# Turning q, k and the softmax's weights of one encoder layer by VectorE and DRAM transfers in place of TensorE

## The chip, the core and the metric

The kernel runs on one core of a Trainium2 chip. The core has a matrix engine (TensorE, "PE" in the profile; its weight loads are listed apart as "PEld"), VectorE ("DVE"), ScalarE ("ACT"), GpSimd ("POOL") and SyncE ("SP"), which here only issues transfers. On-chip memory is SBUF (128 partitions); TensorE writes to PSUM. The metric is device time in microseconds (us), lower is better. A measurement is the median of several runs.

## The reference, cut to what matters

A bidirectional encoder of two layers, batch 1, 256 tokens, width 2048, all in float32. Each layer is a parallel mixer and a convolutional feed-forward net, both modulated by a conditioning vector:

```python
mod = c_act @ ada_w[l] + ada_b[l]                        # 6 x 2048 values
h = rmsnorm(x, norm_mix[l]) * (1.0 + sc_a) + sh_a
qa, ka, va, qb, kb, vb, ga, gb = split_cols(h @ w_in[l])
qa = rotary_partial(rmsnorm(qa.reshape(B, S, HA, HEAD_DIM), qn_a[l]), pos)
ka = rotary_partial(rmsnorm(ka.reshape(B, S, GA, HEAD_DIM), kn_a[l]), pos)
ya = window_attention(qa, ka, va, sink_a[l]) @ w_proj_a[l]      # 8 heads, 2 kv groups
qb = rmsnorm(qb.reshape(B, S, HB, HEAD_DIM), qn_b[l])
kb = rmsnorm(kb.reshape(B, S, HB, HEAD_DIM), kn_b[l])
yb = neighbourhood_attention(qb, kb, vb, rel_bias_b[l]) @ w_proj_b[l]   # 8 heads
merged = jax.nn.sigmoid(ga) * ya + jax.nn.sigmoid(gb) * yb
x = x + gt_a * (merged @ w_out[l])
h = rmsnorm(x, norm_ffn[l]) * (1.0 + sc_m) + sh_m
u = depthwise_conv(h @ w_up[l], conv_w[l], conv_b[l])
g, v = jnp.split(u, 2, axis=-1)
x = x + gt_m * ((jax.nn.silu(g) * v) @ w_down[l])
```

Both attentions are softmax attention over the 256 tokens with a mask or a bias: with heads of 128, `scores = q k^T`, `p = softmax(scores)`, `o = p v`. TensorE contracts over partitions, so the scores need q and k with the head's 128 values on the partitions, and the output needs p with the keys on the partitions. What the projections give has tokens on the partitions, and so do the scores. Hence q, k and p must be transposed ("turned").

## The kernel before, in words

**Weights.** All weight matrices of a layer lie in DRAM as one stream of 128x128 blocks, in the order of their use. A *unit* is 16 blocks, 1 MB. `unit_steps` loads a unit with one transfer from SyncE's queue (L286, the tile "w", a pool "raw" of four buffers) and splits it into two *halves* of eight blocks. A half is float32 values parted in a rounded part and a rest: ScalarE casts the rounded part (L297), VectorE subtracts it from the value (L298); both land in "hl", a pool of four halves. Each product on TensorE is three matmuls (part x part, rest x part, part x rest).

**Loops.** `features` keeps the result with features on the partitions: per block three matmuls (L314, L315, L316) of 128x256. `tokens` keeps tokens on the partitions: per four blocks six matmuls (L377 to L379) of 128x512. Results lie in PSUM ("ps", "ps_t"), and an evacuation function takes them out.

**The second layer's mixer**, unit by unit: units 0 to 7 hold half of the gate of branch A; units 8 to 43 hold q, k and v in nine token groups of four units each (`QKV_GROUPS`); units 44 to 51 hold the rest of A's gate; units 52 to 59 the projection of A (L403 gates it); units 60 to 75 the gate of B; from 76 on come the projection of B, the output projection and the feed-forward net. Beside it, "aw" loads (L225, the same "raw" buffers and the same queue) with one VectorE reduction each (L226) compute the modulation; a plan (`ADA_PLAN_1`) sets how many are done at which unit.

**A group of q and k.** A token group is four heads of 128 (the k group of A two heads, with v in its other columns, copied out at L896). `qk_rows` squares the rows on ScalarE (L547, one per head and half of the tokens), takes the root (L440 on VectorE, L441 on GpSimd), multiplies it in ("qn", L556), applies the rotation to A's (L571 to L573), and then turns them: `turn` transposes every 128x128 block on TensorE with the identity (L580) into PSUM, and ScalarE copies the result with the norm's gain as scale into "packA" or "packB" (L581). Each part comes some ticks after the one before: `bg.defer` puts a function off to the next tick, and there is a tick at every end of a unit.

**A head.** `attend` is a generator. Scores on TensorE (L607, "sc"); row maximum with mask or bias on VectorE (L610); the negative (L615); exp on ScalarE (L618, sum in the same instruction; A's heads also L621 and L622 for the sink); reciprocal (L624) and scaling (L626). After a yield, four transposes on TensorE (L631) into "tp", which are split as above into "pT" (`split`, L389 on ScalarE and L390 on VectorE; pT has one buffer). After a yield the output on TensorE ("po", L639) and its split into "oA" or "oB" (L641, L642). q, k and v of a head are split likewise (`in_halves`; "qh", "kh", "vh" have one buffer each). "p" has two buffers. A head of B loads its bias into p (L825). `attention` advances every living head by one yield a step; `bg.tick` calls it with a rate per unit, `ATT[1]` = 0.4 steps up to the projection of A and `ATT_B[1]` = 0.21 from there on. `attended(HA)` drives the A heads to their end before the projection of A, and `bg.finish(job)` the B heads before unit 76.

**What sets the order.** Every engine takes its instructions from a queue in order, and so does SyncE with the transfers. The order in a queue is not that of the program text: a planner arranges the instructions when the kernel is built, by dependences, by priorities (program order, where nothing else is said) and by its own estimate of each instruction's time. On the chip the queues are then served in that fixed order, with semaphores between them.

Of the kernel before, what the change touches and what calls it, by code (L numbers as in the profile page):

```python
# [9 lines left out]
F32 = mybir.dt.float32  # L10
F32R = mybir.dt.float32r
AF = mybir.ActivationFunctionType
# [3 lines left out]
P = 128  # L16
L = 2
D = 2048
S = 256
KC = D // P  # L20
HEAD = 128
HA, GA, HB = 8, 2, 8
# [5 lines left out]
NEG = -1e30  # L28
SCALE = HEAD ** -0.5
GRID_W, NA_KH, NA_KW = 64, 8, 16  # L30


QKV_GROUPS = [1024, 0, 512, 2560, 3584, 1536, 3072, 4096, 2048]
# [45 lines left out]
H_RATE = [2.7, 1.7]  # L79

ATT = [1.288, 0.4]
ATT_B = [0.21, 0.21]

SCORES_3 = (1,)

ADA_ORDER = [[p * KC + k for k in range(KC) for p in ps] for ps in ((0, 1), (2,), (3, 4), (5,))]
ADA_ORDER = [i for part in ADA_ORDER for i in part]
# [47 lines left out]
def encoder(ctx: ExitStack, tc: tile.TileContext, a: dict, out: bass.AP):  # L135
# [16 lines left out]
    sm = pool("sm", 3)  # L152
    mm = pool("mm", 4, space=bass.MemoryType.PSUM)
    ax = pool("ax", 3, space=bass.MemoryType.PSUM)

    ident = const.tile([P, P], F32, name="ident")
    make_identity(nc, ident[:])
# [378 lines left out]
            nc.vector.tensor_tensor(out=z[:], in0=ps[:, :S], in1=self.rbs[:], op=ALU.mult)  # L536
            return z, sh

    def qk_rows(pss, heads, rot, gain, dst, then):

        cols = 0
        n = heads * HEAD
        ss = sm.tile([P, 8], F32, name="qss", tag="qss")
        for t, ps in enumerate(pss):
            for i in range(heads):
                sq = at.tile([P, HEAD], F32, name="qsq", tag="qsq", bufs=1)
                nc.scalar.activation(  # L547
                    out=sq[:], in_=ps[:, cols + i * HEAD : cols + (i + 1) * HEAD], func=AF.Square,
                    accum_out=ss[:, t * heads + i : t * heads + i + 1],
                )  # L550
        rs = sm.tile([P, 8], F32, name="qrs", tag="qrs")
        rsqrt(rs[:, : 2 * heads], ss[:, : 2 * heads], HEAD, 2 * heads)
        def norm():
            qn = at.tile([P, 2, 4, HEAD], F32, name="qn", tag="qn", bufs=1)
            for t, ps in enumerate(pss):
                nc.vector.tensor_tensor(  # L556
                    out=qn[:, t, :heads],
                    in0=ps[:, cols : cols + n].rearrange("p (h d) -> p h d", d=HEAD),
                    in1=rs[:, t * heads : (t + 1) * heads].unsqueeze(2).broadcast_to([P, heads, HEAD]),
                    op=ALU.mult,  # L560
                )
# [12 lines left out]
            bg.defer(lambda: turn(qn))  # L574

        def turn(qn):
            for t in range(2):
                ps = ax.tile([P, 4, P], F32, name="qtp", tag="ax")
                for h in range(heads):
                    nc.tensor.transpose(ps[:, h], qn[:, t, h], ident[:])  # L580
                nc.scalar.activation(  # L581
                    out=dst[:, :, t * P : (t + 1) * P], in_=ps[:, :heads], func=AF.Identity, scale=gain
                )
            then()

        bg.defer(lambda: bg.defer(lambda: bg.defer(norm)))
# [12 lines left out]

        return ((0, 0), (0, 1), (1, 0))[: 2 * len(x) - 1]  # L600

    def attend(q, k, v, p, mask, scale, sink, o):

        sc = ax.tile([P, 2, S], F32, name="sc", tag="ax")
        for t in range(2):
            for i, j in by(q):
                nc.tensor.matmul(sc[:, t], q[i][:, t * P : (t + 1) * P], k[j], start=i + j == 0, stop=(i, j) == by(q)[-1])  # L607
        m = sm.tile([P, 2], F32, name="m", tag="m")
        for t in range(2):
            nc.vector.tensor_tensor_reduce(  # L610
                out=p[:, t], in0=sc[:, t], in1=mask[:, t], scale=scale, scalar=-3.0e38 if sink is None else sink,
                op0=ALU.add, op1=ALU.max, accum_out=m[:, t : t + 1],
            )
        nm = sm.tile([P, 2], F32, name="nm", tag="nm")
        nc.vector.tensor_scalar(out=nm[:], in0=m[:], scalar1=-1.0, scalar2=None, op0=ALU.mult)  # L615
        den = sm.tile([P, 2], F32, name="den", tag="den")
        for t in range(2):
            nc.scalar.activation(out=p[:, t], in_=p[:, t], func=AF.Exp, bias=nm[:, t : t + 1], accum_out=den[:, t : t + 1])  # L618
# [5 lines left out]
        nc.vector.reciprocal(out=ri[:], in_=den[:])  # L624
        for t in range(2):
            nc.scalar.activation(out=p[:, t], in_=p[:, t], func=AF.Copy, scale=ri[:, t : t + 1])  # L626
        yield
        tp = ax.tile([P, 2, S], F32, name="tp", tag="ax")
        for k in range(2):
            for t in range(2):  # L630
                nc.tensor.transpose(tp[:, k, t * P : (t + 1) * P], p[:, t, k * P : (k + 1) * P], ident[:])  # L631
        pT = at.tile([P, 2, 2, S], F32R, name="pT", tag="pT", bufs=1)
        split(pT, tp[:])
        v = v()
        yield
        po = ax.tile([P, 512], F32, name="po", tag="ax")
        for i, j in by(v):
            for b in range(2):
                nc.tensor.matmul(po[:, :S], v[i][:, b], pT[:, j, b], start=i + j + b == 0, stop=i + b == 2)  # L639
        o = o()  # L640
        nc.scalar.copy(o[:, 0], po[:, :S])  # L641
        nc.vector.tensor_tensor(out=o[:, 1], in0=po[:, :S], in1=o[:, 0].bitcast(F32), op=ALU.subtract)  # L642
# [115 lines left out]
    for l in range(L):  # L758
# [41 lines left out]
        def head_a(i):  # L800
            g = i // (HA // GA)
            if i >= 6:
                oA.append(paired(F32R, f"oA{l}_{i}"))
            elif i % 2 == 0:
                o = place(("y0", "y1", "y2")[i // 2], 4, F32R, f"oA{l}_{i}")
                oA.extend((o[:, :2], o[:, 2:]))
            q = in_halves(qTa[:, i], f"qA{l}_{i}", "qh", l in SCORES_3)
            if i % (HA // GA) == 0:
                kvs[0] = in_halves(kTa[:, g], f"kA{l}_{g}", "kh", l in SCORES_3)
            k = kvs[0]  # L810
            yield
            p = at.tile([P, 2, S], F32, name="p", tag="p")

            def v():
                if i % (HA // GA) == 0:
                    kvs[1] = in_halves(packs[0][:, 1:4:2, g * HEAD : (g + 1) * HEAD], f"vA{l}_{g}", "vh", True)
                return kvs[1]

            yield from attend(q, k, v, p, tables[0], SCALE, sink[:, i : i + 1], lambda: oA[i])

        def head_b(hb):
            b, i = packs[1 + hb // 4], hb % 4
            v = b[:, 4:8].rearrange("p (t a) s -> p t (a s)", t=2)
# [5 lines left out]
            yield from attend(  # L829
                q, k, lambda: in_halves(v[:, :, i * HEAD : (i + 1) * HEAD], f"vB{l}_{hb}", "vh", True), p, p, 1.0, None,  # L830
                lambda: oB_of(hb),
            )

        def oB_of(hb):
# [36 lines left out]
        for pi, (groups, gates) in enumerate(parts):  # L871
            last = pi == len(parts) - 1
            for g, part in enumerate(groups):
# [21 lines left out]
                    for t in range(2):  # L895
                        nc.scalar.copy(rows[:, t, vcol:], pss[t][:, vcol:])  # L896
                if g == 0:
                    qk_rows(pss, GA, rots[1], gains[:, 1:2], kTa, turned)
                elif g < 3:
                    qk_rows(pss, 4, rots[0], gains[:, 0:1], dst, turned)  # L900
                elif vcol is None:
                    qk_rows(pss, 4, None, gains[:, 3:4] if g in (3, 6) else gains[:, 2:3], dst, turned)
                else:
                    turned()
                if g == 2:
# [243 lines left out]
```

## Time and profile before

| | before |
|---|---|
| median of three runs | 2663.79 us (2663.64 to 2665.55) |
| the profiled execution, its span | 2663.2 us |
| TensorE busy | 2650.9 us |
| VectorE busy | 2102.2 us |
| ScalarE busy | 1412.8 us |
| GpSimd busy | 36.2 us |
| traffic with DRAM | 697 MB read and written through the transfer queue, 71.4% of 16 DMA engines |
| granted TensorE clock | full in each of 40 slices |

The profiled execution's own time is its span, 2663.2 us; that is 0.6 us under the median of the runs. The second layer's mixer up to the last B head lies at about 1394 to 1806 us of the span. In the rows below, "out<-in" gives the tiles by their names in the program, "x24" is the number of instructions, and after a bar come the busy time of the group, the mean of one in ns and the idle time just before them, with what ended most of it. In a row of a chain or of a timeline, the first two numbers are start and length in us; a bracket gives the idle time ahead and what ended it.

### The profile page before, as it was taken

Reading aid. Unit: us, or ns where it says so; the run is one execution under the profiler, and the core shown is the slowest. Engines: PE = TensorE matmul, PEld = TensorE weight load, DVE = VectorE, ACT = ScalarE, POOL = GpSimd, SP = SyncE. Lnnn points to the kernel's source line nnn. Section 1 sums busy time; section 2 is a strip of 40 time slices with the busy share of each in tenths; the row PEclk is TensorE's granted clock in tenths of the full one; section 3 lists DMA queues with packets and bytes.
Section 4 is the critical chain, followed back from the end, with each engine's and each line's share of the span. In section 5 each row is a group of like instructions: output and inputs, shape, how many; then the busy total and the mean of one; then the engine's idle time right before and its main releaser. Section 6 shows DMA issues by size and latency. Waiting matters only on the chain.

```text
span 2663.2 us, 50845 instructions
## 1 busy us (share of the span) xinstructions
PE 2650.9 (100%) x21256; PEld 2565.7 (96%) x21256; DVE 2102.2 (79%) x2959; ACT 1412.8 (53%) x2284; POOL 36.2 (1%) x25
## 2 busy tenths in 40 slices
PE   9999999999999999999999999999999999999999
PEld 7888899999999999999998889999999999999999
DVE  8898998997987888788976667768888866655664
ACT  5445865456644555355555566554565445544553
POOL 0001100000000000000000000000000000000000
PEclk9999999999999999999999999999999999999999
DMA  9987789885787878788766666666747765555554
GB/s 372 351 327 292 262 300 352 317 320 199 291 294 287 302 288 295 289 294 289 290 217 254 228 229 231 245 252 253 285 173 288 297 256 190 190 194 194 197 191 143
DMA packets 102039, 700.41 MB, mean 263 GB/s; under 512 B 12721, under 2 KB 15025, under 8 KB 17969
## 3 DMA queue, kind: packets, MB, share of 16 engines
q1 hardware_dynamic: 101810, 697.17, 71.4%
q8 instruction: 166, 2.72, 0.4%
q14 instruction: 63, 0.52, 0.1%
HBM read 695.03 MB, written 2.10 MB: 262 GB/s over the span
## 4 chain that ended last, share of the span: by engine, by line
PE 89%; DVE 6%; ACT 1%; issue 1%; DMA 1%; POOL 0%; SPq 0%; DVEq 0%; ACTq 0%
PE ps L314 25%; PE ps L316 25%; PE ps L315 25%; PE ps_t L377 4%; PE ps_t L379 4%; PE ps_t L378 4%; DVE hl L298 2%; DVE aw L226 2%; DMA aw<-in_aw 1%; PE sc L607 1%; PE po L639 1%; ACT hl L297 1%; PE tp L631 1%; POOL qrs L441 0%; PE qtp L580 0%
## 5 line engine op out<-in xcount | busy, mean ns | idle before, releaser
L298 DVE TENSOR_TENSOR hl<-w,hl 128x1024 fp32r<-128x1024 f32 x928 | 1128.3, 1222 | 360.0 <-ACT hl L297 357.6
L297 ACT CAST hl<-w 128x1024 fp32r<-128x1024 f32 x928 | 970.7, 1049 | 748.5 <-PE ps L316 518.1
L314 PE MATMUL ps<-h,hl 128*128 128x256 f32 x3328 | 922.8, 277 | 1.3 <-DVE ya L915 0.6
L315 PE MATMUL ps<-h,hl 128*128 128x256 f32 x3328 | 919.8, 276 | 0.0
L316 PE MATMUL ps<-h,hl 128*128 128x256 f32 x3328 | 919.8, 277 | 0.0
L314 PEld LDWEIGHTS ps<-h,hl 128*128 128x128 f32 x3328 | 624.8, 188 | 2.4 <-DVE ya L915 0.8
L315 PEld LDWEIGHTS ps<-h,hl 128*128 128x128 f32 x3328 | 625.3, 188 | 0.4 <-DVE h L470 0.2
L316 PEld LDWEIGHTS ps<-h,hl 128*128 128x128 f32 x3328 | 624.4, 188 | 0.0
L226 DVE CUSTOM_DVE_ANT_0 aw<-aw,cact,ab 128x2048 f32<-128x2048 f32 x189 | 443.5, 2347 | 48.8 <-DMA aw<-in_aw 47.8
L377 PE MATMUL ps_t<-hl,h 128*128 128x512 f32 x576 | 223.1, 392 | 2.6 <-ACT h L469 2.1
L378 PE MATMUL ps_t<-hl,h 128*128 128x512 f32 x576 | 224.9, 391 | 0.3
L379 PE MATMUL ps_t<-hl,h 128*128 128x512 f32 x576 | 224.3, 390 | 0.0
L994 DVE SCALAR_TENSOR_TENSOR u<-ps,cw,u 128x255 f32<-128x255 f32 x304 | 146.1, 481 | 66.5 <-ACT u L992 62.2
L992 ACT ACTIVATE u<-ps,cw 128x256 f32<-128x256 f32 x152 | 85.9, 565 | 187.9 <-PE ps L316 187.5
L316 PE MATMUL ps<-merged,hl 128*128 128x256 f32 x512 | 141.8, 277 | 0.4 <-DVE hl L298 0.4
L315 PE MATMUL ps<-merged,hl 128*128 128x256 f32 x512 | 141.6, 277 | 0.0
L314 PE MATMUL ps<-merged,hl 128*128 128x256 f32 x512 | 141.6, 277 | 0.0
L315 PE MATMUL ps<-act_o,hl 128*128 128x256 f32 x512 | 141.4, 276 | 0.0
L316 PE MATMUL ps<-act_o,hl 128*128 128x256 f32 x512 | 141.3, 276 | 0.0
L314 PE MATMUL ps<-act_o,hl 128*128 128x256 f32 x512 | 141.2, 276 | 0.0
L377 PEld LDWEIGHTS ps_t<-hl,h 128*128 128x128 f32 x576 | 107.9, 188 | 26.1 <-ACT h L469 3.1
L378 PEld LDWEIGHTS ps_t<-hl,h 128*128 128x128 f32 x576 | 108.1, 188 | 23.7 <-DVE hl L298 1.9
(231 smaller groups left out, 4612.5 us busy)
## 6 DMA issues: line engine op xcount, KB each, us to landing
w<-in_ws SPq DMA_DIRECT2D x463, 1024.0 KB, 4.9
aw<-in_aw SPq DMA_DIRECT2D x189, 1024.0 KB, 6.1
p<-in_bias SPq DMA_DIRECT2D x16, 256.0 KB, 4.2
x<-in_xT SPq DMA_DIRECT2D x4, 512.0 KB, 5.3
aw_o<-in_aw SPq DMA_DIRECT2D x2, 1024.0 KB, 12.3
out<-x SPq DMA_DIRECT2D x16, 128.0 KB, 2.1
w<-in_ws SPq DMA_DIRECT2D x2, 512.0 KB, 11.7
aw_b<-in_aw SPq DMA_DIRECT2D x1, 1024.0 KB, 18.1
```

The costliest lines, as they stand in the source:

```text
L226: nc.vector.tensor_tensor_reduce(out=raw[:], in0=raw[:], in1=cact[:], scale=1.0, scalar=ab[:, i : i + 1], op0=ALU.mult, op1=ALU.add, accum ...
L297: nc.scalar.copy(hl[:, 0], r)
L298: nc.vector.tensor_tensor(out=hl[:, 1], in0=r, in1=hl[:, 0].bitcast(F32), op=ALU.subtract)
L314: nc.tensor.matmul(out, hi, act[0], start=first, stop=False)
L315: nc.tensor.matmul(ps[:, :S], hi, act[1], start=False, stop=False)
L316: nc.tensor.matmul(out, lo, act[0], start=False, stop=last)
L377: nc.tensor.matmul(ps[:], xh, hi, start=kc == kcs[0], stop=False)
L378: nc.tensor.matmul(ps[:], xh, lo, start=False, stop=False)
L379: nc.tensor.matmul(ps[:], xl, hi, start=False, stop=kc == kcs[-1])
L607: nc.tensor.matmul(sc[:, t], q[i][:, t * P : (t + 1) * P], k[j], start=i + j == 0, stop=(i, j) == by(q)[-1])
L992: nc.scalar.activation(out=u, in_=ps, func=AF.Identity, scale=w[:, 1:2], bias=w[:, 3:4])
L994: nc.vector.scalar_tensor_tensor(out=u[:, to], in0=ps[:, of], scalar=w[:, j : j + 1], in1=u[:, to], op0=ALU.mult, op1=ALU.add)
```

## The change

In the second layer (`MOVED = (1,)`) neither q and k nor p go through TensorE for the turning; the first layer keeps its transposes.

VectorE's `transpose` turns each 32x32 block of a tile within itself. What is left is to move whole blocks to their places. `scatter` writes one 32-partition band of such a tile to a scratch tile in DRAM, 32 values (128 bytes) at a time, so that the tile in DRAM is the full transpose; then one transfer loads it back. A q or k group takes two VectorE turns of 128x512 (128x256 for the k group), eight scatters and one load into its place in "pack", on SyncE's queue, and then one ScalarE scaling with the gain instead of two copies from PSUM. A head takes one VectorE turn of 128x512, eight scatters and one load into the place of pT's rest; the split into pT then reads SBUF in place of PSUM. The load back and the scaling are each put off by a further tick; in a head there is one more yield, ahead of the load. The rate of the heads past the projection of A, `ATT_B[1]`, goes from 0.21 to 0.32 steps a unit. The scratch tiles come from a pool of two buffers per tag.

```diff
-ATT_B = [0.21, 0.21]
+ATT_B = [0.21, 0.32]
+BLOCK = 32
+MOVED = (1,)
...
+    dram = pool("dram", 2, space=bass.MemoryType.DRAM)
...
+    def scatter(y, src, t, a):
+        rows = y[:].rearrange("(b i) n (t a j) -> t a i n b j", i=BLOCK, t=2, a=P // BLOCK)
+        nc.sync.dma_start(rows[t, a], src[a * BLOCK : (a + 1) * BLOCK])
...
         def turn(qn):
+            if moved:
+                flat = qn[:, :, :heads].rearrange("p t h d -> p t (h d)")
+                for t in range(2):
+                    nc.vector.transpose(out=flat[:, t], in_=flat[:, t])
+                y = dram.tile([P, heads, S], F32, name="qY", tag="qY")
+                for t in range(2):
+                    for a in range(4):
+                        scatter(y, qn[:, t, :heads].rearrange("p h (b j) -> p h b j", j=BLOCK), t, a)
+                def back():
+                    nc.sync.dma_start(dst, y[:])
+                    def scaled():
+                        nc.scalar.activation(out=dst, in_=dst, func=AF.Identity, scale=gain)
+                        then()
+                    bg.defer(scaled)
+                bg.defer(back)
+                return
...
+    def once(fn):
+        due = [fn]
+        def run():
+            if due:
+                due.pop()()
+        return run
...
-        tp = ax.tile([P, 2, S], F32, name="tp", tag="ax")
-        for k in range(2):
+        if moved:
+            flat = p[:].rearrange("p t k -> p (t k)")
+            nc.vector.transpose(out=flat, in_=flat)
+            y = dram.tile([P, 2, S], F32, name="pY", tag="pY")
             for t in range(2):
-                nc.tensor.transpose(tp[:, k, t * P : (t + 1) * P], p[:, t, k * P : (k + 1) * P], ident[:])
-        pT = at.tile([P, 2, 2, S], F32R, name="pT", tag="pT", bufs=1)
-        split(pT, tp[:])
+                for a in range(4):
+                    scatter(y, p[:, t].rearrange("p (k b j) -> p k b j", k=2, j=BLOCK), t, a)
+            yield
+            pT = at.tile([P, 2, 2, S], F32R, name="pT", tag="pT", bufs=1)
+            whole = pT[:, 1].bitcast(F32)
+            nc.sync.dma_start(whole, y[:])
+            halve = once(lambda: split(pT, whole))
+            bg.defer(halve)
+        else:
...
         v = v()
         yield
+        if moved:
+            halve()
         po = ax.tile([P, 512], F32, name="po", tag="ax")
...
-            yield from attend(q, k, v, p, tables[0], SCALE, sink[:, i : i + 1], lambda: oA[i])
+            yield from attend(q, k, v, p, tables[0], SCALE, sink[:, i : i + 1], lambda: oA[i], l in MOVED)
...
-                    qk_rows(pss, 4, rots[0], gains[:, 0:1], dst, turned)
+                    qk_rows(pss, 4, rots[0], gains[:, 0:1], dst, turned, l in MOVED)
```

The branch under `else:` in `attend` is the old one. The call sites of B's heads and of the other groups get the same last argument.

More of the change, by code (lines that the diff above doesn't have):

```diff
@@ L537, in level, with qk_rows @@
             return z, sh
-    def qk_rows(pss, heads, rot, gain, dst, then):
+    def scatter(y, src, t, a):
+        rows = y[:].rearrange("(b i) n (t a j) -> t a i n b j", i=BLOCK, t=2, a=P // BLOCK)
+        nc.sync.dma_start(rows[t, a], src[a * BLOCK : (a + 1) * BLOCK])
+    def qk_rows(pss, heads, rot, gain, dst, then, moved=False):
         cols = 0
@@ L600, in by, with attend @@
         return ((0, 0), (0, 1), (1, 0))[: 2 * len(x) - 1]
-    def attend(q, k, v, p, mask, scale, sink, o):
+    def once(fn):
[4 more added lines that the diff above has]
+        return run
+    def attend(q, k, v, p, mask, scale, sink, o, moved=False):
         sc = ax.tile([P, 2, S], F32, name="sc", tag="ax")
@@ L627, in attend @@
         yield
-        tp = ax.tile([P, 2, S], F32, name="tp", tag="ax")
-        for k in range(2):
+        if moved:
+            flat = p[:].rearrange("p t k -> p (t k)")
+            nc.vector.transpose(out=flat, in_=flat)
+            y = dram.tile([P, 2, S], F32, name="pY", tag="pY")
             for t in range(2):
-                nc.tensor.transpose(tp[:, k, t * P : (t + 1) * P], p[:, t, k * P : (k + 1) * P], ident[:])
-        pT = at.tile([P, 2, 2, S], F32R, name="pT", tag="pT", bufs=1)
-        split(pT, tp[:])
+                for a in range(4):
[7 more added lines that the diff above has]
+        else:
+            tp = ax.tile([P, 2, S], F32, name="tp", tag="ax")
+            for k in range(2):
+                for t in range(2):
+                    nc.tensor.transpose(tp[:, k, t * P : (t + 1) * P], p[:, t, k * P : (k + 1) * P], ident[:])
+            pT = at.tile([P, 2, 2, S], F32R, name="pT", tag="pT", bufs=1)
+            split(pT, tp[:])
         v = v()
         yield
+        if moved:
+            halve()
         po = ax.tile([P, 512], F32, name="po", tag="ax")
@@ L830, in head_b @@
                 q, k, lambda: in_halves(v[:, :, i * HEAD : (i + 1) * HEAD], f"vB{l}_{hb}", "vh", True), p, p, 1.0, None,
-                lambda: oB_of(hb),
+                lambda: oB_of(hb), l in MOVED,
             )
@@ L897, in encoder @@
                 if g == 0:
-                    qk_rows(pss, GA, rots[1], gains[:, 1:2], kTa, turned)
+                    qk_rows(pss, GA, rots[1], gains[:, 1:2], kTa, turned, l in MOVED)
                 elif g < 3:
-                    qk_rows(pss, 4, rots[0], gains[:, 0:1], dst, turned)
+                    qk_rows(pss, 4, rots[0], gains[:, 0:1], dst, turned, l in MOVED)
                 elif vcol is None:
-                    qk_rows(pss, 4, None, gains[:, 3:4] if g in (3, 6) else gains[:, 2:3], dst, turned)
+                    qk_rows(pss, 4, None, gains[:, 3:4] if g in (3, 6) else gains[:, 2:3], dst, turned, l in MOVED)
                 else:
```

## The prediction

> **What bounds the kernel now.** The page comes first: busy time, then the slices.
>
> ```profile
> span 2663.2 us, 50845 instructions
> PE 2650.9 (100%) x21256; PEld 2565.7 (96%) x21256; DVE 2102.2 (79%) x2959; ACT 1412.8 (53%) x2284; POOL 36.2 (1%) x25
> PEclk9999999999999999999999999999999999999999
> ```
>
> TensorE is idle for 12.3 us of the span and at full clock in every slice. So time is lost only where TensorE loses it, and what is taken off TensorE is won if nothing makes it wait. The next views are the chain that ended last (start, length, what) around one head of the second layer, and one chain row of the feature loops:
>
> ```profile
> 1536.41 0.71 PE po L639 x6
> 1537.12 0.44 PE tp L631 x4
> 1537.55 0.70 PE sc L607 x6
> 1538.26 0.23 PE ps_t L377
> 1794.03 0.11 PE ps L316
> ```
>
> Four turns of a head's weights hold TensorE 0.44 us, 0.11 each. A half unit is 12 matmuls of 0.23 in the token loops (2.75 us) and 24 of 0.11 in the feature loops (2.7 us). Why does TensorE never wait, though it needs ScalarE and VectorE for every half? The timeline of ScalarE at the same head:
>
> ```profile
> 1536.44 1.05 ACT L297 CAST hl<-w 128x1024 fp32r<-128x1024 f32 x1 [1.21 <-PE ps_t L379]
> 1537.40 0.37 ACT L641 CAST oA<-po 128x256 fp32r<-128x256 f32 x1
> 1541.04 1.05 ACT L297 CAST hl<-w 128x1024 fp32r<-128x1024 f32 x1 [2.34 <-PE ps_t L379]
> 1543.83 0.91 ACT L626 ACTIVATE p<-p,ri 128x256 f32<-128x256 f32 x2 [0.49 <-DVE ri L624]
> ```
>
> The cast at 1536.44 belongs to the second half of unit 34; TensorE has just finished unit 32. The queue of ScalarE thus holds four finished halves before it takes up the copy that waits for this head, and the next cast waits for a free buffer, not for the head. I call this the lead: halves split before an instruction that reads TensorE's result, less the halves TensorE used before it made that result. Read off the built program's queues for units 0 to 79 of the second layer, the lead before the change is 3 to 5 for all 137 such instructions of ScalarE and 2 to 5 for all 112 of VectorE. A lead of 4 hides about 11 us.
>
> **What the change takes from TensorE.** The turns by line, in the stretch that holds those of the second layer (L580, then L631):
>
> ```profile
> 1436.00:1800.00 364.00, 6.81 (x52) 6.05 (x52) 1.00 0.65 238
> 1436.00:1800.00 364.00, 9.64 (x64) 7.35 (x64) 1.00 0.65 238
> ```
>
> All 116 leave TensorE's queue: 116 x 0.11 = 12.8 us, all of it on the path. That is the whole possible gain.
>
> **What it adds.** VectorE gets 28 turns of 128x512 and 2 of 128x256 (two per q/k group, one per head). No row shows this operation. It lies between a 128x256 and a 128x1024 operation, 0.42 and 1.22; I take 0.65, the row of the same size (L556 below): 19 us in all. ScalarE's 14 copies from PSUM become 7 scalings, a few us less; the split of pT reads SBUF and stays. SyncE gets 8 scatters and one load back per group and head: 23 x 9 = 207 issues, some 68 us on a queue that mostly waits:
>
> ```profile
> 1503.25 0.33 SPq L225 DMA_DIRECT2D aw<-in_aw  x1
> w<-in_ws SPq DMA_DIRECT2D x70, 1024.0 KB, 5.0
> aw<-in_aw SPq DMA_DIRECT2D x23, 1024.0 KB, 4.8
> p<-in_bias SPq DMA_DIRECT2D x8, 256.0 KB, 3.4
> q1 hardware_dynamic: 436, 0.40, 8.6%
> ```
>
> The first is SyncE's timeline; the next three are DMA issues in 1394 to 1810 us; the last is the DMA queue in 2650 to 2663.3, nearly alone with 1 KB writes: 8.6% of 16 engines x 13.3 us over 436 packets is 42 ns a packet. The scatters write 59,392 packets of 128 B (4096 a group of four heads, 2048 a head or the k group). A packet costs between its share by bytes, 5 ns, and 42 ns; that is 0.7 to 5.4 us for a head's scatter and 1.4 to 10.8 us for a group's. I take 13 ns, nearer the bytes since no row shows a fixed cost so high. [...]
>
> Behind the scatters queue the weight loads. 93 loads in 416 us through four buffers is 17.9 us a turn; less 5.0 of landing and some 4 of splitting, a load can come about 9 us late. At 13 ns a scatter with its issues takes 4.3 to 6 us: covered, save where the lead is gone. I add 7 us for that; the ends are 0 and 45 (seven groups 4.5 us over the cover at 42 ns, the rest at heads 8 and 9).
>
> **What it moves.** This decides. The built program of the changed kernel has another order: in the same units the lead is 0 for 26 of 107 instructions on ScalarE and 44 of 96 on VectorE. At unit 37, for one:
>
> ```
> TensorE  37 second half | po | sc | 38 first half
> VectorE  37 second half | pT | oA<-po | aw | max<-sc x2 | qA | nm | 38 first half
> ```
>
> VectorE takes half 38 only after it has the head's output and scores, which TensorE makes after the last half it has. TensorE stands still for the rest of that chain, whatever the transfers do. Each place costs its chain less what TensorE does meanwhile (po and sc 1.4). Prices, ScalarE and VectorE in 1394 to 1810 us, then GpSimd:
>
> ```profile
> L297 ACT CAST hl<-w 128x1024 fp32r<-128x1024 f32 x139 | 145.6, 1048 | 128.4 <-PE ps_t L379 78.6 <-PE ps L316 49.8
> L618 ACT ACTIVATE p<-p,nm 128x256 f32<-128x256 f32 x32 | 16.0, 500 | 3.9 <-DVE nm L615 3.9
> L547 ACT ACTIVATE qsq<-ps_t 128x128 f32<-128x128 f32 x52 | 14.5, 279 | 5.1 <-PE ps_t L379 4.2
> L547 ACT ACTIVATION_READ_ACCUMULATOR qsq<-ps_t 128x1 f32 x52 | 10.4, 199 | 0.0
> L389 ACT CAST pT<-tp 128x512 fp32r<-128x512 f32 x16 | 9.5, 595 | 0.0
> L618 ACT ACTIVATION_READ_ACCUMULATOR p<-p,nm 128x1 f32 x32 | 6.0, 187 | 0.0
> L389 ACT CAST qA<-packA 128x256 fp32r<-128x256 f32 x8 | 3.3, 416 | 0.1
> L896 ACT COPY packB<-ps_t 128x512 f32<-128x512 f32 x4 | 2.4, 588 | 2.2 <-PE ps_t L379 2.0
> ```
>
> ```profile
> L298 DVE TENSOR_TENSOR hl<-w,hl 128x1024 fp32r<-128x1024 f32 x140 | 170.4, 1223 | 102.9 <-ACT hl L297 102.5
> L226 DVE CUSTOM_DVE_ANT_0 aw<-aw,cact,ab 128x2048 f32<-128x2048 f32 x24 | 56.4, 2348 | 8.5 <-DMA aw<-in_aw 8.4
> L390 DVE TENSOR_TENSOR pT<-tp,pT 128x512 fp32r<-128x512 f32 x16 | 10.9, 682 | 0.1
> L556 DVE TENSOR_TENSOR qn<-ps_t,qrs 128x512 f32<-128x512 f32 (+1 forms) x14 | 8.5, 648 | 11.5 <-POOL qrs L441 11.5
> L610 DVE CUSTOM_DVE_ANT_0 p<-sc,maskA,sink 128x256 f32<-128x256 f32 x16 | 7.0, 478 | 2.0 <-PE sc L607 2.0
> L403 DVE SCALAR_TENSOR_TENSOR ya<-ya,ps 128x256 f32<-128x256 f32 x16 | 6.6, 414 | 2.6 <-PE ps L316 2.6
> L642 DVE TENSOR_TENSOR oA<-po,oA 128x256 fp32r<-128x256 f32 x8 | 3.3, 418 | 0.2 <-ACT oA L641 0.2
> L390 DVE TENSOR_TENSOR qA<-packA,qA 128x256 fp32r<-128x256 f32 x8 | 3.4, 421 | 0.5 <-ACT qA L389 0.5
> L610 DVE DVE_READ_ACCUMULATOR2_ANT m<- 128x1 f32 x32 | 2.6, 82 | 0.0
> L615 DVE TENSOR_SCALAR nm<-m 128x2 f32<-128x2 f32 x16 | 2.6, 161 | 0.0
> ```
>
> ```profile
> L441 POOL TENSOR_TENSOR qrs<-qss,mhalf 128x8 f32<-128x8 f32 (+1 forms) x14 | 30.0, 2143 | 540.3 <-DVE qss L440 540.3
> ```
>
> Short names: cast 1.05, rest 1.22, max 0.56 (a pair 1.12), exp 0.69, squares 3.83 (eight), roots 2.14, qn 1.30 (two), turn 1.30 (two), aw 2.43, one half of a q, k or v 0.42 on either engine, o 0.42, small ones 0.16. After the second half of unit:
> - 24: max, half, sc, max, qn, turn, two small, exp, cast, rest: 8.4 less 1.5 = 6.9.
> - 27: two copies 1.18, cast, rest = 3.5.
> - 31: squares, small, roots, qn, turn, two small, rest: 10.3 less two halves = 4.8.
> - 34: po and sc, max, half, small, half, rest: 4.4 less 1.4 = 3.0.
> - 35: squares, small, roots, qn, turn, rest = 9.9, with nothing beside it.
> - 37: po, o, aw, max pair, half, small, rest: 6.5 less 1.4 = 5.1.
> - 39: copies, pT cast and rest, po and sc, two halves, max pair, two exp, four small, scaling 0.45, cast, rest: 10.6 less 1.4 = 9.2.
> - 42: 1.4.
> - 43 to 44: squares among cast, exps, pT and scalings 7.9, small, roots, qn, turn 4.9, o, max pair, halves, rest 3.8: 16.6 less 6.8 = 9.8.
> - 47: gate copy, pT, po and sc, three halves, max, rest: 4.7.
> - 49: po, o, aw, max pair, half, small, exp, cast, rest: 6.8.
> - 51: the last A heads are driven to their end here, so two heads follow each other, and the load back of head 8 waits for head 7's po (pT has one buffer): 10.6 less 2.8 = 7.8.
> - 52: 3.0. 55 and 58: gated copy and rest, 1.2 each. 59: 1.9.
>
> Sum 80.2. An unseen turn at 0.42 or 1.22 moves it by -2 or +5.
>
> **The sum.** 80.2 - 12.8 + 7 = 74.4 on the profiled 2663.2 us gives 2737.6; the median of the runs, 2663.79, stands 0.6 above that span: 2738.
>
> **Rivals.**
> Faster: the lead lives on although the queues read otherwise. Then only the 12.8 us count: 2651. It decides where the fifteen places together cost under 12.8, under 0.9 us each. For it speaks TensorE's record now; against it, that a queue is served in order and cast plus rest alone are 2.3 us. Chance 0.03; within 0.2% 0.02.
> Smaller chains: parts of them run earlier than I place them, and half is lost, 40 us: 2691 with no late transfers. Chance 0.08.
> Late transfers: packets at 42 ns add 38 us to the 7: 2776. For it speaks that nothing here shows a 128 B write; against it, the 9 us of cover. Chance 0.16.
> Half clock: a TensorE that stands still is slowed afterwards. At the start it was slow:
>
> ```profile
> 9.69 3.50 PE L410 MATMUL warm<-ident 128*128 128x128 f32 x16
> 13.39 2.92 PE L410 MATMUL warm<-ident 128*128 128x128 f32 x24
> ```
>
> 0.22 a matmul, then 0.12: sixteen lost 1.6 us. Ten places of 3.5 us or more would lose 16: 2754. Against it, no gap now says when it begins. [...] Chance 0.16.
> That the turns stay on TensorE is out: its queue holds none.
>
> **How the numbers follow.** My own case has 0.55 and 2738, alone 2710 to 2765. The range reaches down to half the chains and up over the late transfers with part of the slow clock: 2690 to 2800, leaving out some 0.1. A measurement of this kernel can tell 0.2% from no change. Faster 0.03, same 0.02, slower 0.95.
>
> **What would show it.** No L580 or L631 rows in the second layer; TensorE idle some 80 us between 1480 and 1780, named by hl on VectorE or ScalarE, longest at units 35, 39, 44 and 51; turns near 0.65; scatters landing within 6 us. Wrong if the gaps are ended by DMA instead, if the clock row falls, or if TensorE stays full.

## The result and the profile after

The changed kernel takes 2742.12 us (median of four runs, 2739.74 to 2742.55) against 2663.93 for the kernel before: a ratio of 1.0289, 95% interval 1.0275 to 1.0302. It is slower by 78 us. The forecast was 2738, slower.

From the page of the changed kernel: span, busy time, then clock and transfers.

```profile
span 2740.2 us, 50974 instructions
PE 2671.0 (97%) x21140; PEld 2573.1 (94%) x21140; DVE 2118.1 (77%) x2989; ACT 1411.6 (52%) x2277; POOL 35.4 (1%) x25
PEclk9999999999999999999999988999999999999999
q1 hardware_dynamic: 167586, 712.39, 71.9%
```

TensorE is idle for 2740.2 - 2671.0 = 69.2 us, 56.9 more than before. It is also busy for 2671.0 us, although its 116 turns are gone. Without them it should be 2650.9 - 12.8 = 2638.1, so 32.9 us went into matmuls that took longer, and the clock row shows two slices under full speed. 56.9 + 32.9 - 12.8 = 77.0 is the whole difference of the spans.

Where is it idle? The windows below lie around its stalls in the second layer's mixer: bounds, width, then busy time of TensorE, its weight loads, VectorE, ScalarE and GpSimd, the granted clock, the transfers' share of 16 engines and their GB/s.

```profile
1486.50:1496.00 9.50, 5.31 (x21) 3.48 (x19) 6.12 (x19) 5.80 (x13) 0.33 (x1) 0.80 0.80 296
1514.50:1518.50 4.00, 1.86 (x8) 0.91 (x7) 1.92 (x2) 3.91 (x6) 0.00 (x0) 1.00 0.00 0
1545.00:1548.00 3.00, 0.57 (x3) 0.14 (x3) 3.00 (x7) 2.26 (x5) 0.00 (x0) 1.00 0.99 403
1559.50:1563.50 4.00, 1.73 (x9) 1.04 (x8) 3.75 (x11) 3.67 (x9) 0.00 (x0) 1.00 0.70 193
1569.50:1579.00 9.50, 2.00 (x6) 1.02 (x6) 4.64 (x7) 8.12 (x22) 1.64 (x1) 0.74 0.23 98
1593.00:1599.00 6.00, 1.75 (x6) 1.01 (x6) 5.95 (x11) 4.40 (x9) 0.00 (x0) 0.91 0.48 89
1610.00:1619.00 9.00, 2.48 (x15) 1.87 (x14) 3.20 (x11) 5.29 (x13) 0.00 (x0) 0.97 0.47 130
1638.50:1640.50 2.00, 0.74 (x4) 0.34 (x3) 2.00 (x4) 1.29 (x2) 0.00 (x0) 1.00 0.57 164
1652.50:1659.00 6.50, 1.68 (x10) 1.28 (x9) 6.22 (x14) 4.99 (x12) 0.25 (x1) 0.77 0.88 282
1676.50:1683.00 6.50, 2.91 (x19) 2.11 (x18) 3.67 (x8) 4.36 (x8) 0.00 (x0) 1.00 0.26 57
1696.50:1703.50 7.00, 1.36 (x6) 0.86 (x6) 5.65 (x12) 3.85 (x10) 0.00 (x0) 0.78 0.40 78
1717.50:1727.00 9.50, 4.11 (x19) 3.31 (x17) 6.75 (x21) 6.58 (x16) 0.00 (x0) 0.82 0.89 314
1735.00:1738.50 3.50, 1.31 (x8) 0.91 (x6) 2.62 (x7) 3.01 (x6) 0.00 (x0) 0.92 0.88 332
1759.50:1761.50 2.00, 0.82 (x7) 0.62 (x7) 1.99 (x4) 1.05 (x1) 0.00 (x0) 1.00 0.52 66
1779.00:1781.00 2.00, 0.80 (x7) 0.59 (x7) 2.00 (x4) 0.00 (x0) 0.00 (x0) 1.00 0.74 185
1787.00:1790.00 3.00, 1.21 (x8) 0.81 (x7) 2.79 (x6) 3.00 (x5) 0.00 (x0) 1.00 1.01 423
sum 87.00, PE 30.64 PEld 20.30 DVE 62.28 ACT 61.56 POOL 2.21; mean PE 1.91 PEld 1.27 DVE 3.89 ACT 3.85 POOL 0.14
```

In these sixteen stretches TensorE is idle for 87.00 - 30.64 = 56.4 us, which is nearly all of the 56.9. They follow, in this order, the second halves of units 24, 27, 32, 34, 35, 37, 39, 42, 44, 47, 49, 51, 52, 55, 58 and 59.

What ends the stalls is seen at unit 37, whose order the prediction wrote out. The timelines of ScalarE and of VectorE there:

```profile
1592.55 0.37 ACT L695 CAST oA<-po 128x256 fp32r<-128x256 f32 x1 [14.71 <-PE po L693]
1593.25 0.41 ACT L393 CAST qA<-packA 128x256 fp32r<-128x256 f32 x1 [0.33 <-PE sc L645]
1593.56 1.99 ACT L301 CAST hl<-w 128x1024 fp32r<-128x1024 f32 x2
```

```profile
1592.95 0.42 DVE L696 TENSOR_TENSOR oA<-po,oA 128x256 fp32r<-128x256 f32 x1 [10.80 <-ACT oA L695]
1593.29 2.34 DVE L230 CUSTOM_DVE_ANT_0 aw<-aw,cact,ab 128x2048 f32<-128x2048 f32 x1
1596.37 0.42 DVE L394 TENSOR_TENSOR qA<-packA,qA 128x256 fp32r<-128x256 f32 x1
1596.92 2.36 DVE L302 TENSOR_TENSOR hl<-w,hl 128x1024 fp32r<-128x1024 f32 x2
```

ScalarE stands still for 14.71 us ahead of the copy of a head's output, and VectorE for 10.80, with the next halves queued behind it. In the kernel before, such a copy at 1537.40 was reached with four finished halves ahead. The cast at 1593.56 waits for no transfer: it follows the copy and one split at once. Nor are the stalls ended by transfers elsewhere: the waits of TensorE between 1480 and 1800 us all end with ScalarE or VectorE, and between 1394 and 1900 us ScalarE's casts wait for weight loads only three times (what waited, for what; us in total, times, longest):

```profile
ACT hl L301 <- DMA w<-in_ws: 4.4, 3, 1.9
```

### The profile page after: what moved, and what is told of

Read it like the earlier page. It is cut to its first block, busy times and chain, and to the rows that moved or that the text cites. A ratio compares the mean times of both kernels' runs of the same rounds, so it can differ in the third digit from the quotient of the medians.

```text
span 2740.2 us, 50974 instructions
## 1 busy us (share of the span) xinstructions
PE 2671.0 (97%) x21140; PEld 2573.1 (94%) x21140; DVE 2118.1 (77%) x2989; ACT 1411.6 (52%) x2277; POOL 35.4 (1%) x25
## 5 line engine op out<-in xcount | busy, mean ns | idle before, releaser
L382 PE MATMUL ps_t<-hl,h 128*128 128x512 f32 x576 | 230.0, 400 | 12.5 <-DVE hl L302 12.0
L381 PE MATMUL ps_t<-hl,h 128*128 128x512 f32 x576 | 225.2, 399 | 16.0 <-ACT hl L301 14.4
L383 PE MATMUL ps_t<-hl,h 128*128 128x512 f32 x576 | 228.2, 397 | 0.0
```

Of the source, the lines that this page charges most:

```text
L381: nc.tensor.matmul(ps[:], xh, hi, start=kc == kcs[0], stop=False)
L382: nc.tensor.matmul(ps[:], xh, lo, start=False, stop=False)
L383: nc.tensor.matmul(ps[:], xl, hi, start=False, stop=kc == kcs[-1])
```

## The experiments

All kernels are compared with the kernel before on the same chip. TensorE's idle time is the span less its busy time; "slow" is its busy time less what is due, 2650.9 us with the turns and 2638.1 without (not all of it is a slower clock, as is shown further below).

| kernel | median us | ratio to before (95%) | TensorE idle | slow |
|---|---|---|---|---|
| before | 2663.93 | 1 | 12.3 | 0 |
| changed | 2742.12 | 1.0289 (1.0275 to 1.0302) | 69.2 | 32.9 |
| scatter_gpsimd | 2797.92 | 1.0503 (1.0487 to 1.0518) | 118.4 | 38.0 |
| weights_gpsimd | 2700.94 | 1.0141 (1.0126 to 1.0156) | 43.7 | 17.2 |
| dead_scatter | 2725.39 | 1.0230 (1.0213 to 1.0247) | 44.9 | 27.3 |
| dead_gpsimd | 2730.50 | 1.0250 (1.0235 to 1.0265) | 61.7 | 17.3 |
| pinned | 2711.11 | 1.0158 (1.0135 to 1.0180) | 52.9 | 17.7 |
| pinned_late | 2715.45 | 1.0174 (1.0155 to 1.0194) | 57.9 | 16.2 |
| no_transfers | 2657.11 | 0.9964 (0.9951 to 0.9977) | 12.5 | -0.7 |
| no_turning | 2655.03 | 0.9949 (0.9931 to 0.9966) | 14.5 | 0.6 |
| pinned_back_in_p | 2719.55 | 1.0195 (1.0178 to 1.0213) | 58.9 | 20.6 |
| pinned_weights_scalar | 2724.00 | 1.0210 (1.0193 to 1.0227) | 58.9 | 28.0 |
| dead_tiny | 2666.09 | 1.0003 (0.9993 to 1.0013) | 12.5 | 0.2 |
| dead_pinned | 2675.46 | 1.0042 (1.0029 to 1.0055) | 19.2 | 4.6 |

The "lead" is that of the prediction: halves split ahead, in a queue, of an instruction that reads TensorE's result. In each group of runs the kernel before was run anew: its medians were 2664.37 for the four runs next below, 2667.78 for pinned to no_turning, 2666.18 for the two after these, 2664.69 for the last two.

### Another queue for the scatters, or for the weights

```diff
-        nc.sync.dma_start(rows[t, a], src[a * BLOCK : (a + 1) * BLOCK])
+        nc.gpsimd.dma_start(rows[t, a], src[a * BLOCK : (a + 1) * BLOCK])
-                    nc.sync.dma_start(dst, y[:])
+                    nc.gpsimd.dma_start(dst, y[:])
-            nc.sync.dma_start(whole, y[:])
+            nc.gpsimd.dma_start(whole, y[:])
```

> The changed kernel with all 184 scatters and 23 load backs issued from GpSimd's queue in place of SyncE's; nothing else differs. In the built program the lead is back: 0 nowhere, 3 to 5 for 106 of 107 such instructions of ScalarE and 1 to 5 on VectorE. Order theory (the stalls come from the order that the planner made when it saw the scatters ahead of the weight loads on one queue): TensorE is idle about 12 us as before, clock full, 12.8 us of turns gone, so 2651, at most 2660, faster than before. Transfer theory (59,392 packets of 128 bytes take time on the DMA engines, weight loads land late): the same packets flow, so it stays at 2720 or more. Issue theory (the 207 issues hold up SyncE's queue): 2651 as well.

It took 2797.92 us. That lies where the transfer theory put it, but not for its reason: on GpSimd's queue the transfers went in 8,112 packets, against 65,776 more packets on SyncE's in the changed kernel, and the weight loads between 1480 and 1800 us landed in 5.3 us in the median, as in the kernel before. The order and the issue theory missed. Its waits between 1394 and 1900 us:

```profile
ACT pT L393 <- DMA pT<-pY: 118.5, 15, 21.0
POOL qY L546 <- issue: 122.5, 43, 6.2
```

GpSimd spends some 3 us (122.5 over 43) between one scatter of a q or k group and the next, so a load back comes so late that a lead of 3 to 5 halves does not outlast it: ScalarE waits up to 21.0 us for one. My lead had counted only readers of TensorE's results; a reader of a load back stands in the same queue.

```diff
-            nc.sync.dma_start(raw[:], a["ws"][l, u])
+            (nc.gpsimd if l and 18 <= u < 76 else nc.sync).dma_start(raw[:], a["ws"][l, u])
```

> The changed kernel with the scatters left on SyncE's queue, and instead the weight and aw loads of units 18 to 75 of the second layer issued from GpSimd's. The lead is 1 to 6 everywhere. Order theory: 2651 to 2665, no stall over 2 us in units 18 to 60. Transfer theory: 2720 or more. Issue theory: 2651 to 2665, since no weight load stands behind a scatter.

(The aw loads likewise.) 2700.94 us: 41 of the 78 us came back, and no theory had put it there. What is left shows in its timeline of ScalarE:

```profile
1527.69 1.15 ACT L601 ACTIVATE packB<-packB,gains 128x1024 f32<-128x1024 f32 x1 [12.87 <-DMA packB<-qY]
```

The scaling of a q or k group was put ahead of the next cast, and its load back is not there yet.

### The scatters alone, with nothing that reads them

```diff
+        if moved:
+            y = dram.tile([P, 2, S], F32, name="pY", tag="pY")
+            for t in range(2):
+                for a in range(4):
+                    scatter(y, p[:, t].rearrange("p (k b j) -> p k b j", k=2, j=BLOCK), t, a)
         tp = ax.tile([P, 2, S], F32, name="tp", tag="ax")
```

(and likewise in `turn` of a q or k group).

> The kernel before, TensorE's turns kept, with the 184 scatters added on SyncE's queue; what they write is never read, and there is no load back. The built order has lost the lead (0 for 36 of 137 instructions on ScalarE and 41 of 112 on VectorE). Order theory: TensorE stands still as in the changed kernel, 50 to 70 us, with slow matmuls after the longer stalls, 25 to 40, and the 12.8 us of turns are still paid: 2740 to 2775. Transfer theory: 2740 to 2775 too. A theory in which the readers of the scratch tiles (load back, then split, then output) make the stalls: no stall, 2664 to 2670.

> As the run before, but the unread scatters are issued from GpSimd's queue. The built order has the lead of the kernel before (3 to 5 on ScalarE, 2 to 6 on VectorE). Order theory: 2664 to 2672, the price of the packets by themselves. Transfer theory: 2740 to 2775, as with SyncE's queue.

2725.39 and 2730.50 us. The stalls do not need the load backs: the scatters alone cost 61 us on SyncE's queue, some 15 us under the 2740 to 2775 that the order and the transfer theory gave. The sister on GpSimd's queue was meant to price the packets with the lead alive. It could not, since the same bytes went in 5,888 packets there and in 62,336 on SyncE's queue, and it was spoiled by its queue besides, as its waits show:

```profile
DVE qn L565 <- POOL qrs L445: 65.5, 7, 20.5
```

The roots of q and k are computed by GpSimd, and stand in line behind the scatters there; before, the seven of this stretch were waited for by 11.5 us in all (its group row for L556 stands in the prediction). So moving the transfers to GpSimd decides nothing about order or packets, and a cleaner pair was needed.

### The order tied

Two units are split ahead in the program's text, and all other instructions of the mixer's ticks and evacuations are tied behind the newest half of their queue, in order of issue only:

```diff
+                if self.l and 8 <= self.u < 74:
+                    self.prefetch(2 - len(self.ahead))
...
+    def behind(l, u):
+        s = ExitStack()
+        if l and 8 <= u < 76:
+            for i in newest:          # newest cast and newest subtraction
+                s.enter_context(tc.issue_after(i.ins))
+        return s
...
-            bg.tick()
+            with behind(self.l, self.u):
+                bg.tick()
```

> The changed kernel, every instruction and transfer on its own queue as there, but two units are split ahead and the other instructions of ScalarE and VectorE are tied behind the newest half of their queue (order of issue only, no wait). The lead is 1 to 6 on ScalarE and 1 to 6 or 10 on VectorE, 0 nowhere. Order theory alone: the stalls go, 2651 to 2665. Joint theory, formed from the run with the weights on GpSimd's queue (the order costs about half, and a load back that lands later than the lead lasts costs the rest, by the reader of the load back that stands in ScalarE's queue): 2680 to 2710, TensorE's waits named by instructions behind pT or pack from their load back. Transfer theory (weight loads late by the packets): 2730 or more.

> As pinned, and the reader of a load back is put off: the scaling of a q or k group by two more ticks, the split of pT by one more. Order theory alone: as pinned. Joint theory: faster than pinned by 10 to 40 us, 2655 to 2685, since the load backs have landed when their readers are reached; what is left is the drive of the A heads before the projection of A. Transfer theory: no change against pinned.

2711.11 and 2715.45 us. With the lead restored (and two units split ahead, which is part of the edit), the change costs 43 us in place of 78, so the tied order wins back some 35 here. Putting off the readers of the load backs gave nothing: that part of the joint theory fell. What ends the stalls of pinned is another thing. The casts, which waited 4.4 us for weight loads in the changed kernel, now wait far longer in the same stretch:

```profile
ACT hl L310 <- DMA w<-in_ws: 102.2, 28, 10.9
```

Its queue of SyncE, and ScalarE at the same place:

```profile
1599.82 4.00 SPq L559 DMA_DIRECT2D qY<-qn  x6
1603.93 5.16 SPq L559 DMA_DIRECT2D pY<-p  x8
1609.14 0.60 SPq L609 DMA_DIRECT2D packB<-qY  x1
1609.78 0.90 SPq L299 DMA_DIRECT2D w<-in_ws  x2
```

```profile
1616.14 1.99 ACT L310 CAST hl<-w 128x1024 fp32r<-128x1024 f32 x2 [10.90 <-DMA w<-in_ws]
```

Two weight loads leave after fourteen scatters and a load back, and ScalarE has waited 10.90 us for the first of them when it casts at 1616.14.

Two further attempts went at this queue. One loads back into the head's own p, which frees SyncE from waiting for the head before:

```diff
-            whole = pT[:, 1].bitcast(F32)
+            whole = p[:]
```

> As pinned, but the load back of a head goes into the head's own p, not into pT, so that it no longer waits on SyncE's queue until the output of the head before has read pT (this wait is 25 us in pinned and 47 us in the changed kernel). Queue theory, formed from the profile of pinned (the stalls left there end with a weight load that stood on SyncE's queue behind scatters and load backs that wait for their data): 2690 to 2705, 5 to 20 us off the 2711 of pinned; the waits for a turn (58 us for p, 34 us for qn) remain. Order theory alone: as pinned, 2711. Packet theory: as pinned.

The other issues the weight and aw loads from ScalarE's queue, with this and with the late readers:

```diff
-            nc.sync.dma_start(raw[:], a["ws"][l, u])
+            (nc.scalar if l and 18 <= u < 76 else nc.sync).dma_start(raw[:], a["ws"][l, u])
```

> Pinned order, load back into p, its readers put off as in pinned_late, and the weight and aw loads of units 18 to 75 issued from ScalarE's queue, so that none of them stands behind a scatter; the scatters stay on SyncE's. Queue theory together with order theory: both causes are gone, 2651 to 2670, TensorE idle 12 to 20 us, clock 0.99 or more. Packet theory (the 59,392 packets delay the weight loads on the DMA engines): 2695 or more, weight loads landing over 7 us after their issue. A loss of another kind: the 77 issues, 0.33 us each, stand in front of casts on ScalarE; with a lead of 4 halves they cost nothing.

2719.55 and 2724.00 us: neither is better than pinned, and the queue theory fell as a cure. The second lies where the packet theory put it (2695 or more), but without its sign: its weight loads between 1480 and 1800 us landed in 5.9 us in the median, not in over 7. In both profiles ScalarE still waits for weight loads; in the second, between 1480 and 1800 us:

```profile
ACT hl L311 <- DMA w<-in_ws: 63.0, 20, 7.0
ACT p L671 <- DVE nm L668: 41.2, 10, 10.9
```

The second row is a wait in the queue that now issues the weight loads, so some of them may leave late there; that was not shown.

### The turning alone, and nothing at all

no_transfers leaves out scatters, scratch tiles and load backs; no_turning is the kernel before without the 116 transposes:

```diff
-        tp = ax.tile([P, 2, S], F32, name="tp", tag="ax")
-        for k in range(2):
-            for t in range(2):
-                nc.tensor.transpose(tp[:, k, t * P : (t + 1) * P], p[:, t, k * P : (k + 1) * P], ident[:])
+        tp = p
```

> The changed kernel without scatters, scratch tiles and load backs: the VectorE turns stay, and the scaling and the split of pT read the turned tiles themselves, so that the blocks stay in the wrong places. The built order has its lead (3 to 5, 1 to 6). Order theory and joint theory: 2651 to 2655, the whole gain of 12.8. If the 30 turns on VectorE or the moved copies cost something on the path: above 2655.

> The kernel before with the 116 transposes of the second layer left out and nothing in their place: the copies and splits read qn and p unturned. All theories: 2664 less 12.8 = 2651; it prices the term of the sum that the change wins. If less comes out, the turns on TensorE were partly hidden.

2657.11 and 2655.03 us, against 2667.78 in this group, whose runs of the kernel before spread more widely than elsewhere (2664.22 to 2677.04). The turns are worth 2667.78 - 2655.03 = 12.75 us on TensorE, as worked out (9 to 18 by the interval of the ratio); in the profiles TensorE's busy time falls from 2650.9 to 2638.7, by 12.2. The turns on VectorE take 2 us of that or nothing, since the intervals overlap. So moving the turns off TensorE is right by itself, and all the loss is in what carries the blocks. no_transfers also keeps the rate of 0.32 and the added yield and ticks of the change, so these by themselves cost nothing that shows.

### Issues, packets, order

The last pair keeps the kernel before and its turns. dead_tiny puts an issue at the place of every scatter, behind the same data, with 32 writes of 8 bytes:

```diff
-        nc.sync.dma_start(rows[t, a], src[a * BLOCK : (a + 1) * BLOCK])
+        nc.sync.dma_start(y[a * BLOCK : (a + 1) * BLOCK, 0, t * P : t * P + 2], src[a * BLOCK : (a + 1) * BLOCK, 0, 0, :2])
```

dead_pinned is dead_scatter with the tied order of pinned.

> The kernel before with 184 issues added on SyncE's queue at the places of the scatters, each behind the same data, but each writes only 32 times 8 bytes that nobody reads. The built order keeps its lead (3 to 5 and 2 to 6). Queue theory (standing in line behind a transfer that waits for its data, and the issues themselves, make the weight loads late): TensorE idle 20 to 40 us more than before, 2680 to 2705. Packet theory (the time of the 128 byte packets, at issue or on the DMA engines, makes them late): 2664 to 2670. Order theory: 2664 to 2670.

> The kernel before with the full scatters of 128 bytes on SyncE's queue, unread, and the order tied as in pinned, so that the lead is 1 to 10, 0 nowhere; dead_scatter is the same with the lead lost, at 2725. Queue theory: as dead_tiny, 2680 to 2705. Packet theory: 2690 to 2715, well above dead_tiny. Order theory: 2664 to 2675.

From the pages of dead_scatter, dead_pinned and dead_tiny, in this order:

```profile
span 2723.1 us, 51122 instructions
PE 2678.2 (98%) x21256; PEld 2581.3 (95%) x21256; DVE 2102.4 (77%) x2959; ACT 1414.3 (52%) x2284; POOL 38.1 (1%) x25
q1 hardware_dynamic: 164146, 704.79, 71.5%
```

```profile
span 2674.7 us, 51129 instructions
PE 2655.5 (99%) x21256; PEld 2566.9 (96%) x21256; DVE 2099.3 (78%) x2959; ACT 1411.9 (53%) x2284; POOL 36.4 (1%) x25
```

```profile
span 2663.6 us, 51158 instructions
PE 2651.1 (100%) x21256; PEld 2565.6 (96%) x21256; DVE 2100.9 (79%) x2959; ACT 1410.2 (53%) x2284; POOL 37.0 (1%) x25
```

184 issues on SyncE, each waiting in line for p or qn, cost nothing that shows: 1.4 us, with an interval on both sides of none. Eight of them hold SyncE for 3.55 us at the least, where eight full scatters hold it for 5.16 in the row of pinned, so they do not price the whole holding time. The queue theory falls here, for issues alone. The full scatters with the lead kept cost 10.8 us. The same scatters with the lead lost cost 61.0. So the order is 50 of the 61 us, and it is the planner's order: by its built queues dead_tiny keeps the lead untied, dead_scatter does not, and between them only the size and number of the writes differ. (dead_pinned differs from dead_scatter also in that units are split ahead in the program's text; the two were not tried apart.)

## Why the prediction was right

**The turns, 12.8 us.** Right: 12.75 by no_turning.

**VectorE's turns, 0.65 each, off the path.** Right. Their group rows in the changed kernel, 20.2 us in all where 19 was forecast; in no_transfers they cost 2 us or nothing:

```profile
L668 DVE STREAM_TRANSPOSE p<-p 128x512 f32<-128x512 f32 x16 | 11.3, 709 | 4.5 <-ACT p L664 4.3
L589 DVE STREAM_TRANSPOSE qn<-qn 128x512 f32<-128x512 f32 (+1 forms) x14 | 8.9, 658 | 0.0
```

**The issues, 0.33 each.** Mis-sized: eight scatters hold SyncE for 5.16 us in the row of pinned, 0.65 each, twice the 0.33 of a weight load. The conclusion that a queue that mostly waits bears it holds for issues alone (dead_tiny, 1.4 us for 184 of them).

**The packets, 13 ns, and 7 us for late loads.** Right in size. dead_scatter moved 164,146 - 101,810 = 62,336 packets more than the kernel before on this queue, and 71.5% of 2723.1 us less 71.4% of 2663.2 is 45.5 us of 16 engines: 12 ns a packet. dead_pinned, with the same packets and 73.0% of 2674.7 us, gives 13. It prices the scatters at 10.8 us, and in the changed kernel the casts waited 4.4 us for weight loads. The upper end of 42 ns, measured on 1 KB writes, is not seen in these writes. In the changed kernel the weight loads landed later than before; the issues of the kernel before and of the changed one between 1480 and 1800 us:

```profile
w<-in_ws SPq DMA_DIRECT2D x52, 1024.0 KB, 5.3
```

```profile
w<-in_ws SPq DMA_DIRECT2D x39, 1024.0 KB, 7.0
```

In dead_scatter, with the scatters but without load backs, they landed in 5.3 us in the same stretch.

**The order, 80.2 us.** The mechanism and the places were right: 15 of the 16 places named are stalls (the first rival counts fifteen places where sixteen are listed); the one after unit 31 (4.8 us) is none, and one after unit 32 (2.43) was not named. Of the four that were to be longest, 35, 39 and 51 are among the four longest; 44 is the fifth. The size was too large: 56.4 - 2.4 = 54.0 us at the fifteen places, for which 75.4 were forecast. At unit 37, 5.1 were forecast, and TensorE was idle for 6.00 - 1.75 = 4.25: it began half 38 with the cast alone while VectorE still had the rest to do. Two chains were also added a little high by their own prices, 8.4 for 8.1 at unit 24 and 4.4 for 4.2 at unit 34. Where the rest of the 21 us went was not traced. dead_scatter against dead_pinned shows the cause on the chip, for the scatters alone.

**The half clock.** This was a rival of its own with a chance of 0.16 and 16 us, and a falling clock row was named as a sign that the forecast is wrong. It fell, and beside my own case. This is the step that failed: I had taken the two as exclusive, although in the changed kernel the slow clock came behind my own stalls, and my sum has no term for it. The changed kernel has eleven stretches at a granted clock of 0.50 between 1492 and 1745 us; in the 3.41 us ahead of each, TensorE was idle for 1.83 to 3.41 us. The sum line of their windows, from 1492.16:1498.99 to 1737.92:1744.75, and then the stall after unit 39 with what follows it:

```profile
sum 58.05, PE 46.82 PEld 40.34 DVE 43.58 ACT 35.47 POOL 0.42; mean PE 4.26 PEld 3.67 DVE 3.96 ACT 3.22 POOL 0.04
1610.00:1618.60 8.60, 2.11 (x14) 1.49 (x12) 2.80 (x10) 4.89 (x13) 0.00 (x0) 0.99 0.47 132
1618.60:1621.80 3.20, 3.13 (x7) 2.03 (x8) 3.16 (x4) 3.20 (x4) 0.00 (x0) 0.50 0.14 21
```

TensorE is busy for 46.82 us of these 58.05. My estimate is that this work would have taken half as long at full clock, so that the half clock costs some 23 of the 32.9 us: in the chain a matmul of 128x512 takes 0.43 us at 1620.68, at a clock of 0.50, and 0.23 at 1622.21, at full clock. That leaves 9.5 us of longer matmuls; what made them longer was not shown. In the stall after unit 39 TensorE is idle for 6.5 us, 5.32 of them in one piece, and the clock is 0.50 for the 3.2 us behind it. The half-clock rival counted the places of 3.5 us or more, a bound that no run shows: ahead of one stretch at 0.50 the longest single wait is 1.75 us, as the last section shows.

**The sum.** 80.2 - 12.8 + 7 = 74.4 was forecast; 56.9 of idleness, 32.9 of longer matmuls and -12.8 make 77.0. The time was met, 2738 against 2742, because 87.2 us of stalls (chains and late loads) were forecast and 56.9 came, and the 30 us too many stood in for the 32.9, most of it slow clock, that were left out. The direction and the cause of the stalls were found; the closeness of the number is luck, two misses of about the same size and opposite sign.

**What stays open.** With the lead restored, the full change still costs 43 us, and it saves 12.8 of turns: some 56 us, of which the scatters themselves explain 11. The other 45 come in with the load backs and what waits for them. The rate of the heads was not undone beside the transfers; without them, in no_transfers, it costs nothing. The load back into pT, its readers' place and the queue of the weight loads were each tried as the cause, and none took it away. No version with the transfers beat the kernel before.

## What to carry to other kernels

Where a planner fixes the order of the queues, an edit is priced by the order that it causes as well as by its instructions: count, in the built queues, how many prepared buffers stand ahead of each instruction that reads the bottleneck's result. Here the same scatters cost 11 us with that lead and 61 without. Where stalls are forecast, what comes behind them needs a term of its own: here matmuls at half clock took some 23 us, by the estimate above, beside 57 of stalls.

## What the runs showed of the hardware that was not expected

The slow clock came behind rows of short stalls too, not only behind one long one. Of the eleven stretches at a granted clock of 0.50 in the changed kernel, six last 3.41 us, four 6.83 and one 10.24. Two of them, each with the 3.41 us ahead of it, and last a stretch that none followed:

```profile
1488.75:1492.16 3.41, 1.37 (x8) 0.83 (x6) 2.65 (x11) 2.45 (x7) 0.00 (x0) 1.00 1.01 425
1492.16:1498.99 6.83, 5.13 (x12) 3.59 (x13) 5.19 (x11) 5.30 (x11) 0.00 (x0) 0.50 0.54 100
1560.43:1563.84 3.41, 1.55 (x6) 0.98 (x7) 3.41 (x9) 3.41 (x9) 0.00 (x0) 1.00 0.64 140
1563.84:1567.25 3.41, 3.41 (x10) 2.63 (x9) 1.21 (x4) 0.91 (x2) 0.00 (x0) 0.50 0.46 75
1611.63:1615.04 3.41, 1.67 (x12) 1.47 (x12) 2.18 (x6) 0.68 (x2) 0.00 (x0) 1.00 0.31 82
```

TensorE is idle for 2.04, 1.86 and 1.74 us of the stretches in the first, the third and the last row, and its longest single wait in the third is 1.75 us. The clock was 0.50 behind the first two and full behind the last. No bound follows from these numbers: between 1545.00 and 1547.80 us TensorE was idle for 2.35 us, and the clock was full there and from 1548 to 1551. What sets the clock was not shown.

And the transfers issued by GpSimd were dear for GpSimd's other work: with 184 scatters on its queue in dead_gpsimd the roots were waited for by 65.5 us in place of 11.5, though the bytes were those of SyncE's queue (7.6 MB). Part of it is the pauses between the scatters of q and k, in which it waits for nothing that the profile shows (128.1 us in 43 of them), and part is that its queue stands until a scatter's data is there (59.6 us for p, in five waits).
